# Seven-product (Strassen) matrix products for v and half of z, and the layer norm of v in steps beside the conv projections

## Chip, cores and metric

The kernel runs on one core of one Trainium2 chip. The metric is the device time in microseconds (us) of one execution. The engines are TensorE (PE), VectorE (DVE), ScalarE (ACT), GpSimd (POOL) and SyncE (SP, whose queue issues most loads). Each engine takes its instructions strictly in the order in which they stand in its own list.

## The reference, cut to what matters

One layer over T = 1088 tokens: 1024 rows of a prompt and 64 rows of a sample. All arithmetic is float32.

```
h = RMSNorm(x)
u, v, z, xBC, dt, gate_a, gate_b = split(h @ w_in)      # v: 1024 columns, z: 2048, dt: 32
v   = LayerNorm(gelu(v)) * ln_w + ln_b                  # also an output for the sample rows
o_a = gelu(u) * (W_s v + b)                             # 8 groups of 128 channels, W_s 128 x 128 over positions
xs, B, C = silu(causal_conv(xBC))
y   = SSD(xs, softplus(dt + dt_bias), -exp(a_log), B, C) + D * xs
o_b = GroupRMSNorm(y * silu(z))
x  += RMSNorm((sigmoid(gate_a) * (o_a @ w_a) + sigmoid(gate_b) * (o_b @ w_b)) @ w_out)
x  += RMSNorm(relu(RMSNorm(x) @ w_up)^2 @ w_down)
```

## The kernel before

**Products.** Each float32 operand is split into a high part and a low part (`split`, L79 to L81: ACT copies the source to the high part, `wh`, `hTh`; DVE or POOL subtracts it from the source, which leaves the low part, `wl`, `hTl`). A product of two operands is three matmuls, high x high, high x low and low x high, added in PSUM. `h` stands transposed in SBUF as three column blocks `hT` of 384, 384 and 320 tokens.

**z and v.** `proj_M` (L122 to L134) computes one row tile of 128 tokens by 512 weight columns in 8 x 3 = 24 matmuls of 512 columns. The weights of a column group come as four pieces of 512 KB (`raw`, then `wh`, `wl`). There are nine row tiles; the ninth holds the 64 rows of the sample, and takes 24 matmuls as well. z has four column groups, the loop `for gi in range(1, G)` runs over the last three, and v (`v_part`) has two. A z tile is finished by `sz` on ACT (L344) and DVE (L345) and written to `z_d` in DRAM by POOL's queue (L346). A v tile goes through gelu (`gelu2`, L193 to L196, L214), and in the second half of `v_part` through the layer norm (L219 to L227), and is written to `v_d`.

**dt.** `dt_part` is a generator whose pieces stand between the tiles of z group 1: 72 matmuls give dt for all tokens, nine transposes (L262) turn it, a chain of small DVE and ACT operations (L264 to L285, among them a reciprocal, L276) computes the softplus and times `a`, result `q1`; two matmuls (L289, L292) give its running sums `pcum` and the sums that `toend` is made of.

**After v.** The gate projections (`gate_gen`) and the SSD stage follow. In it, each of four groups projects B, C and xs (`xbc_chunk`: `proj_T`, L118 to L120, 24 matmuls of 384 or 320 columns for each of three token blocks, then the conv: ACT L419 takes PSUM into `raw`, DVE L430 three times, DVE L434 once), and runs the blockwise recurrence. The u projection with the spatial mixing (`spatial`), the branches and the FFN come last; the FFN's products (L966 to L968, L1116 to L1118) are already done by seven products each.

**What sets the order.** The code says what depends on what and how many buffers a tile name has (`bufs`); a scheduler then writes out the list of each engine from estimated times. So code that stands next to each other in a loop is interleaved in the lists, and the lists of before and after are shown below where they matter. Memory of a closed pool is used again by the pool opened next, once all work on the old tiles has ended.

## Time and profile before

| | |
|---|---|
| median of 3 runs (lowest to highest) | 2264.83 us (2264.32 to 2266.65) |
| the profiled execution | 2264.54 us, span 2262.7 us |
| mean granted TensorE clock | 0.992 |
| PE busy | 2193.6 us, 97% |
| PE weight load busy | 1966.6 us, 87% |
| DVE, ACT, POOL busy | 58%, 41%, 36% |
| the chain that ended last | PE 67%, issue 12%, POOL 8%, DVE 5% |

The span runs from the first to the last instruction; the 1.8 us beside it are start and end of the execution. "Busy" is the union of an engine's instructions. The chain that ended last follows the last instruction back to what released it, step by step. The stages, by the names of the rows: z and dt up to about 240 us, v to 337, gates to 361, SSD from there to about 1020, u and spatial mixing to 1140, branches to about 1540, FFN to the end.

### The profile page before, as it was taken

Reading aid. Unit: us, or ns where it says so; the run is one execution under the profiler, and the core shown is the slowest. Engines: PE = TensorE matmul, PEld = TensorE weight load, DVE = VectorE, ACT = ScalarE, POOL = GpSimd, SP = SyncE. Lnnn points to the kernel's source line nnn. Section 1 sums busy time; section 2 is a strip of 40 time slices with the busy share of each in tenths; the row PEclk is TensorE's granted clock in tenths of the full one; section 3 lists DMA queues with packets and bytes.
Section 4 is the critical chain, followed back from the end, with each engine's and each line's share of the span. In section 5 each row is a group of like instructions: output and inputs, shape, how many; then the busy total and the mean of one; then the engine's idle time right before and its main releaser. Section 6 shows DMA issues by size and latency. Waiting matters only on the chain.

```text
span 2262.7 us, 33194 instructions
## 1 busy us (share of the span) xinstructions
PE 2193.6 (97%) x12674; PEld 1966.6 (87%) x12674; DVE 1323.5 (58%) x1850; ACT 924.7 (41%) x1788; POOL 818.9 (36%) x798
## 2 busy tenths in 40 slices
PE   8999999999999989999999999998999998999997
PEld 6777778989979979889999999777999997788786
DVE  5322255677677667655722257377555556577777
ACT  5212255445445455433311133255555555433333
POOL 2010163372472562753322555353222223123134
PEclk9999999999999999999999999999999999999999
DMA  5223123253252342442354445453444447534533
GB/s 183 70 84 109 58 84 115 58 144 97 80 138 81 105 125 69 129 126 76 97 173 130 134 119 166 135 172 114 147 152 148 140 148 244 163 116 131 172 119 114
DMA packets 315464, 281.07 MB, mean 124 GB/s; under 512 B 40043, under 2 KB 281389, under 8 KB 314793
## 3 DMA queue, kind: packets, MB, share of 16 engines
q1 hardware_dynamic: 283336, 240.71, 35.8%
...
q14 instruction: 60, 0.48, 0.1%
...
## 4 chain that ended last, share of the span: by engine, by line
PE 67%; issue 12%; POOL 8%; DVE 5%; DMA 4%; ACT 3%; SPq 0%; ACTq 0%; POOLq 0%; DVEq 0%
PE ps L119 8%; PE ps L118 8%; PE ps L120 8%; PE X L968 3%; PE X L966 3%; PE X L967 3%; PE X L1117 3%; PE X L1118 3%; PE X L1116 3%; PE ps L1117 2%; PE ps L1116 2%; PE ps L1118 2%; DMA raw<-w_branch_b 2%; PE ps L706 2%; PE ps L705 2%
## 5 line engine op out<-in xcount | busy, mean ns | idle before, releaser
L118 PE MATMUL ps<-hTh,wh 128*128 128x384 f32 (+1 forms) x1152 | 384.4, 334 | 5.5 <-ACT raw L419 5.5
L120 PE MATMUL ps<-hTh,wl 128*128 128x384 f32 (+1 forms) x1152 | 386.4, 335 | 0.0
L119 PE MATMUL ps<-hTl,wh 128*128 128x384 f32 (+1 forms) x1152 | 384.5, 334 | 0.0
L81 POOL TENSOR_TENSOR wl<-raw,wh 128x1024 fp32r<-128x1024 f32 x74 | 182.4, 2467 | 270.3 <-ACT wh L80 268.0
L80 ACT ACTIVATE wh<-raw 128x1024 fp32r<-128x1024 f32 x128 | 135.3, 1057 | 268.9 <-PE ps L119 98.2
L118 PEld LDWEIGHTS ps<-hTh,wh 128*128 128x128 f32 x1152 | 217.1, 188 | 11.6 <-ACT raw L419 6.0
L120 PEld LDWEIGHTS ps<-hTh,wl 128*128 128x128 f32 x1152 | 216.9, 188 | 9.8 <-issue 9.7
L119 PEld LDWEIGHTS ps<-hTl,wh 128*128 128x128 f32 x1152 | 217.2, 189 | 7.9 <-issue 7.3
L132 PE MATMUL ps<-wh,hTh 128*128 128x512 f32 (+1 forms) x432 | 171.3, 398 | 1.0 <-ACT hTh L177 0.9
L133 PE MATMUL ps<-wl,hTh 128*128 128x512 f32 (+1 forms) x432 | 170.4, 396 | 0.9 <-DVE wl L81 0.9
L134 PE MATMUL ps<-wh,hTl 128*128 128x512 f32 (+1 forms) x432 | 171.0, 396 | 0.2 <-DVE hTl L178 0.2
L430 DVE SCALAR_TENSOR_TENSOR acc<-raw,cw,acc 128x384 f32<-128x384 f32 (+1 forms) x216 | 134.6, 626 | 33.6 <-ACT acc L428 27.7
L966 PE MATMUL X<-hb,wu 128*128 128x272 f32 x512 | 147.7, 291 | 1.9 <-ACT ev L973 1.0
L967 PE MATMUL X<-hb,wu 128*128 128x272 f32 x512 | 147.6, 289 | 0.3 <-DVE hb L790 0.3
L968 PE MATMUL X<-hb,wu 128*128 128x272 f32 x512 | 146.1, 290 | 0.0
L514 ACT ACTIVATE bc<-bc,pcum 128x128 f32<-128x128 f32 (+1 forms) x288 | 90.8, 384 | 89.3 <-POOL bc L511 88.4
L1110 POOL TENSOR_TENSOR wd<-wd,wd 128x1024 f32<-128x1024 f32 x32 | 85.8, 2684 | 113.6 <-DVE dl L81 74.5
L705 PE MATMUL ps<-ob,wh 128*128 128x384 f32 (+1 forms) x384 | 125.4, 327 | 0.0
L706 PE MATMUL ps<-ob,wl 128*128 128x384 f32 (+1 forms) x384 | 125.4, 327 | 0.0
L704 PE MATMUL ps<-ob,wh 128*128 128x384 f32 (+1 forms) x384 | 125.4, 326 | 0.0
L80 ACT ACTIVATE dh<-wd 128x1024 fp32r<-128x1024 f32 x56 | 59.1, 1055 | 153.2 <-PE ps L1117 91.9
L81 DVE TENSOR_TENSOR dl<-xd,dh 128x1024 fp32r<-128x1024 f32 x56 | 100.4, 1818 | 1.8 <-PE X L968 1.2
...
## 6 DMA issues: line engine op xcount, KB each, us to landing
raw<-w_in SPq DMA_DIRECT2D x72, 512.0 KB, 4.0
xd<-rc_d SPq DMA_DIRECT2D x112, 256.0 KB, 3.9
...
bc<-ac_d SPq DMA_DIRECT2D x64, 256.0 KB, 4.1
raw<-w_branch_b SPq DMA_DIRECT2D x32, 512.0 KB, 4.1
wr<-w_up SPq DMA_DIRECT2D x32, 512.0 KB, 4.1
...
```

The lines of the kernel that those rows point to most:

```text
L80: s.activation(hi, src, AF.Copy)
L81: (lo_eng or v).tensor_tensor(out=lo, in0=src, in1=hi, op=ALU.subtract)
L118: pe.matmul(ps[:, :n], wh[:, k, :], hh[:, k, :n], start=(k == 0), stop=False)
L119: pe.matmul(ps[:, :n], wh[:, k, :], hl[:, k, :n], start=False, stop=False)
L120: pe.matmul(ps[:, :n], wl[:, k, :], hh[:, k, :n], start=False, stop=(k == 7))
L132: pe.matmul(ps[:R, :], hh[:, k, o:o + R], wh[:, kk, :], start=(k == 0), stop=False)
L134: pe.matmul(ps[:R, :], hl[:, k, o:o + R], wh[:, kk, :], start=False, stop=(k == 7))
L705: pe.matmul(ps[:, :n], wh[:, k, :], ob[:, 4 + kk, :], start=False, stop=False)
L706: pe.matmul(ps[:, :n], wl[:, k, :], ob[:, kk, :], start=False, stop=(k == 7))
L966: pe.matmul(ps, wh[:, k, :], bh[:, k, :], start=start and k == 0, stop=False, skip_group_check=chain)
L967: pe.matmul(ps, wh[:, k, :], bl[:, k, :], start=False, stop=False, skip_group_check=chain)
L968: pe.matmul(ps, wl[:, k, :], bh[:, k, :], start=False, stop=k == 3, skip_group_check=chain)
```

## The change

- **z groups 0 and 1** stay as they were, but the sample's tile is done by `sample`: high and low part of the 64 rows stand side by side as 128 columns (`xss`), so that 16 matmuls do what 24 did; the two halves of the result are added after one of them has been moved over by an SP transfer (`sample_out`).
- **v (block 0) and z groups 2 and 3 (block 1)** are 1024 columns each, and become two blocks of seven products in the order P2, P1, P6, P5, P7, P3, P4 (`plan`): the 1024 rows of the prompt are taken as two halves of four row tiles, the depth 1024 and the columns 1024 as two halves each. A product is four row tiles of 12 matmuls, with sums of row tiles (`operand`) on one side and sums of weight quarters (`build`) on the other. P1, P6, P7 and P4 add up in four PSUM tiles `X`. The samples' rows go beside them with `sample`.
- **The sums.** e2, e3 and e4 of the row tiles are built in z group 1 (`sums`: POOL adds, DVE subtractions, `split`), e1 in block 0 (`sum_e1`), written over two halves of `hT`, whose old contents are kept in `b12_d` and loaded back after P7 of block 1. The weight sums are POOL additions of 128 x 1024 pieces (`build`), then split (`prep`).
- **Layer norm** of v: a generator `ln_gen` reads a row tile of `v_d`, normalizes it and writes it back, in steps between the conv projections of xs and at the end of each SSD group. Its weight and bias are applied in `spatial` (one more 128 x 128 matmul for each of 8 chunks), and for the sample's output in `ln_gen` itself with four loads through one buffer (`lo`).
- **dt_part** stands at the start of the SSD stage, its later pieces between the B and C projections of the first group.

The core of the diff:

```diff
...
-        def v_part():
...
-        def dt_part(sp, wk):
...
+        def dt_part(wa, wb_, wc, wd):
...
+        def operand(n, m, x):
+            if n in es:
+                return es[n][x][:, :, m * P:m * P + P]
+            return row_op(*((m, 0), (m, 1), (4 + m, 1), (4 + m, 0))[n], x)
...
+        def sample(ps, j, w, start, stop):
...
+            for q in range(4):
+                wh, wl = (x[:, q % 2, :] for x in w(q // 2))
+                xs_ = xss[:, j * 4 + q, :]
+                if q == 0:
+                    pe.matmul(ps, xs_, wh, start=start, stop=False, skip_group_check=True)
+                pe.matmul(ps[:64], xs_[:, 0:64], wl, start=False, stop=False, skip_group_check=True)
+                if q > 0:
+                    pe.matmul(ps, xs_, wh, start=False, stop=stop and q == 3, skip_group_check=True)
...
+        def build(k, q):
...
+            elif n == "P6":
+                t = kept[b, q] = w_piece(b, 1, 1, q, "v2", True)
+                u = w_piece(b, 0, 0, q, "w11", False)
+                tt_(out=t, in0=t, in1=u, op=ALU.subtract)
+                u = w_piece(b, 0, 1, q, "w12", False)
+                tt_(out=t, in0=t, in1=u, op=ALU.add)
...
+                t = w_piece(b, 1, 0, q, "v4", True)
+                tt_(out=t, in0=t, in1=kept[b, q], op=ALU.subtract)
...
+            def sums(m):
...
+                for x, (i, half) in ((x12, (4 + m, 0)), (x11, (m, 0)), (x22, (4 + m, 1)), (x21, (m, 1))):
+                    g.tensor_tensor(out=x, in0=row_op(i, half, 0), in1=row_op(i, half, 1), op=ALU.add)
+                v.tensor_tensor(out=e1, in0=x12, in1=x11, op=ALU.subtract)
+                v.tensor_tensor(out=e2, in0=x22, in1=e1, op=ALU.subtract)
+                v.tensor_tensor(out=e3, in0=x12, in1=x22, op=ALU.subtract)
+                v.tensor_tensor(out=e4, in0=x21, in1=e2, op=ALU.subtract)
+                for n, e in ((4, e2), (5, e3), (6, e4)):
+                    split(e, operand(n, m, 0), operand(n, m, 1))
...
+            for i in range(NT):
+                z_tile(ws, 1, i)
+                if i in (0, 2, 4, 6):
+                    sums(i // 2)
+                if i in (5, 7):
+                    build(0, (i - 5) // 2)
+                if i == 7:
+                    prep(0, 0)
+            prep(0, 1)
...
+            def sum_e1(m):
...
+                for x, i in ((x12, 4 + m), (x11, m)):
+                    g.tensor_tensor(out=x, in0=row_op(i, 0, 0), in1=row_op(i, 0, 1), op=ALU.add)
+                v.tensor_tensor(out=x12, in0=x12, in1=x11, op=ALU.subtract)
+                split(x12, operand(3, m, 0), operand(3, m, 1))
...
+            todo = [lambda m=m: sum_e1(m) for m in range(4)]
...
+            for k, (b, n) in enumerate(plan):
...
+                for m in range(4):
+                    ps = X[m] if chained else mm.tile([P, 512], F32, tag="mm", name="ps")
+                    mms(ps, XN[n], k, m, n == "P1" or not chained, chained)
+                    if m % 2 == 0:
+                        prep(k + 1, m // 2)
+                    else:
+                        build(k + 2, m // 2)
+                        if todo:
+                            todo.pop(0)()
...
+                    elif n == "P1":
+                        v.tensor_tensor(out=cz[m], in0=ps, in1=cz[m], op=ALU.add)
+                        epi(pm, gelu, cz[m], P, out_rows(b, m, 0), True)
+                    elif n == "P6":
+                        c1[m] = s2("c1")
...
+                    else:
+                        epi(pm, gelu, ps, P, out_rows(b, 4 + m, 0), False)
...
+                if n == "P7" and b == 1:
+                    for d, x in b12_parts():
+                        nc.sync.dma_start(out=x, in_=d)
...
+            def ln_gen():
...
+                for i in (8, 0, 1, 2, 3, 4, 5, 6, 7):
+                    R = ROWS[i]
+                    hs_ = [half("la"), half("lb")]
...
+                        nc.sync.dma_start(out=hs_[f][:R], in_=v_d[i * P:i * P + R, f * 512:f * 512 + 512])
+                    yield
...
+                    for f in range(2):
+                        v.tensor_reduce(out=m[:R, f:f + 1], in_=hs_[f][:R], axis=mybir.AxisListType.X, op=ALU.add)
...
+                    for f in range(2):
+                        v.tensor_scalar(out=hs_[f][:R], in0=hs_[f][:R], scalar1=r[:R], scalar2=None, op0=ALU.mult)
+                        nc.sync.dma_start(out=v_d[i * P:i * P + R, f * 512:f * 512 + 512], in_=hs_[f][:R])
...
+                        for f in range(2):
+                            x = hs_[f]
+                            o = sp.tile([P, 4, P], F32, tag="s4", bufs=1, name="lo").rearrange("p a b -> p (a b)")
+                            for name, op in (("gmlp_ln_w", ALU.mult), ("gmlp_ln_b", ALU.add)):
+                                nc.sync.dma_start(out=o[:R], in_=a[name][0, f * 512:f * 512 + 512].partition_broadcast(R))
+                                v.tensor_tensor(out=x[:R], in0=x[:R], in1=o[:R], op=op)
+                            g.dma_start(out=a["new_gmlp_v_sample"][0, 0][:, f * 512:f * 512 + 512], in_=x[:R])
...
+            dtg = dt_part(wa, wb_, wc, wd)
+            next(dtg)
+            lng = ln_gen()
...
                 for t, th in xbc_chunk(16 + gi, lambda t: sp.tile([P, 384], F32, tag="BT", bufs=3, name="BT")):
                     BT.append(th)
+                    next(dtg, None)
...
+                    next(dtg, None)
...
+                        next(lng, None)
...
+                next(lng, None)
+                next(lng, None)
...
+                pe.matmul(tp[:, 0, :], ones, wt, start=True, stop=True)
+                v.scalar_tensor_tensor(out=bs, in0=tp[:, 0, :], scalar=lnc[:, 8 + c:9 + c], in1=bs, op0=ALU.mult, op1=ALU.add)
...
+                    v.scalar_tensor_tensor(out=q[:, :nf * P].rearrange("p (a b) -> p a b", b=P), in0=sm[:, :nf * P].rearrange("p (a b) -> p a b", b=P),
+                                           scalar=lw, in1=bs.unsqueeze(1).to_broadcast([P, nf, P]), op0=ALU.mult, op1=ALU.add)
...
```

Where instructions move, the lists of the engines show it. The names in them are tile names with a buffer number.

**PE, where `q1` meets `tri`** (the first matmul of the running sums of dt). Before, it stands between two z tiles of group 1:

```order
L132 MATMUL ps_842<-wh_624,hTh1_95 128x512
L133 MATMUL ps_842<-wl_625,hTh1_95 128x512
L134 MATMUL ps_842<-wh_624,hTl1_96 128x512
L289 MATMUL ps_871<-q1_795,tri_657 128x288
L292 MATMUL ps_874<-q1_795,ones_660 128x288
L132 MATMUL ps_880<-wh_606,hTh1_95 128x512
L133 MATMUL ps_880<-wl_607,hTh1_95 128x512
L134 MATMUL ps_880<-wh_606,hTl1_96 128x512
```

After the change the same matmul (now L254, weights `wb__2427`, which holds `q1`) stands in the first SSD group, behind the last token block of the B projection (`ps_2626`) and ahead of the C projection (`ps_2682`):

```order
L121 MATMUL ps_2626<-hTh2_98,wl_2403 128x320
L119 MATMUL ps_2626<-hTh2_98,wh_2402 128x320
L120 MATMUL ps_2626<-hTl2_99,wh_2402 128x320
L121 MATMUL ps_2626<-hTh2_98,wl_2403 128x320
L254 MATMUL ps_2664<-wb__2427,wa_2426 128x288
L257 MATMUL ps_2667<-wb__2427,wa_2426 128x288
L119 MATMUL ps_2682<-hTh0_94,wh_2676 128x384
L120 MATMUL ps_2682<-hTl0_95,wh_2676 128x384
L121 MATMUL ps_2682<-hTh0_94,wl_2677 128x384
L119 MATMUL ps_2682<-hTh0_94,wh_2676 128x384
```

The matmul moved from the z stage to the start of the SSD stage, and everything behind it on PE, the C projection first, comes after it.

**DVE, the chain that ends in `q1`.** Before, between the reciprocal's input and `q1`, DVE's list holds one operation of another kind (L345, z):

```order
L273 TENSOR_SCALAR q1_795<-d1_794 128x288
L274 TENSOR_TENSOR d1_794<-d1_794,q1_795 128x288
L276 RECIPROCAL d1_794<-d1_794 128x288
L345 SCALAR_TENSOR_TENSOR sz_838<-sz_838,ps_813 128x512
L277 TENSOR_TENSOR u1_793<-u1_793,d1_794 128x288
L278 TENSOR_TENSOR u1_793<-u1_793,q1_795 128x288
L279 TENSOR_TENSOR u1_793<-u1_793,e1_792 128x288
L281 TENSOR_TENSOR dtv_102<-dtv_102,u1_793 128x288
L284 TENSOR_TENSOR q1_795<-dtv_102,dtb_662 128x288
L285 MEMSET q1_795 64x32
```

After, with the reciprocal at L241, the conv (L627, L631) and the layer norm (L669) of the same stage stand between its steps:

```order
L239 TENSOR_TENSOR wb__2427<-wb__2427 128x288
L627 SCALAR_TENSOR_TENSOR acc_2615<-raw_2587,cw_2412,acc_2615 128x384
L241 RECIPROCAL wb__2427<-wb__2427 128x288
L631 SCALAR_TENSOR_TENSOR BT_2553<-BT_2553,acc_2548 128x384
L669 TENSOR_REDUCE lm_3205<-lb_3161 128x1
L627 SCALAR_TENSOR_TENSOR acc_2615<-raw_2587,cw_2412,acc_2615 128x384
L242 TENSOR_TENSOR wb__2427<-wb__2427 128x288
L82 TENSOR_TENSOR wl_3121<-raw_3118,wh_3120 128x1024
L627 SCALAR_TENSOR_TENSOR acc_2656<-raw_2624,cw_2412,acc_2656 128x323
L627 SCALAR_TENSOR_TENSOR acc_2615<-raw_2587,cw_2412,acc_2615 128x384
L243 TENSOR_TENSOR wb__2427<-wb__2427 128x288
L627 SCALAR_TENSOR_TENSOR acc_2656<-raw_2624,cw_2412,acc_2656 128x323
```

The chain kept its steps and got neighbours: from its first step (L229) to `q1` (L249) DVE's list holds 9 operations L627, 3 L631, 2 L669, 2 L683, 1 L692, 1 low part of a weight piece (L82) and 3 copies of 3 columns (L613, L619) besides.

**POOL, in block 0.** Before, at the start of v, POOL has one short operation for each tile (L194, gelu) behind the writes of z:

```order
L346 DMA z_d_80<-sz_1579 128x512
L346 DMA z_d_80<-sz_1608 64x512
L194 TENSOR_SCALAR gq_1678<-gq_1678 128x512
L194 TENSOR_SCALAR gq_1710<-gq_1710 128x512
L194 TENSOR_SCALAR gq_1742<-gq_1742 128x512
L194 TENSOR_SCALAR gq_1774<-gq_1774 128x512
L194 TENSOR_SCALAR gq_1806<-gq_1806 128x512
```

After, beside P1 of block 0, row sums (L485), gelu (L316), weight sums (L365, L367) and writes of v (L321) stand there; `v2_1079` is the second half of P6's weights:

```order
L485 TENSOR_TENSOR x_1088<-hTh1_96,hTl1_97 128x512
L485 TENSOR_TENSOR x_1087<-hTh0_94,hTl0_95 128x512
L321 DMA v_d_81<-cz_1015 128x512
L365 TENSOR_TENSOR v2_1079<-v2_1079,w11_1081 128x1024
L485 TENSOR_TENSOR x_1143<-hTh2_98,hTl2_99 128x512
L321 DMA v_d_81<-cz_1045 128x512
L485 TENSOR_TENSOR x_1142<-hTh0_94,hTl0_95 128x512
L485 TENSOR_TENSOR x_1199<-hTh2_98,hTl2_99 128x512
L316 TENSOR_SCALAR t_1174<-t_1174 128x512
L485 TENSOR_TENSOR x_1198<-hTh1_96,hTl1_97 128x512
L367 TENSOR_TENSOR v2_1079<-v2_1079,w12_1084 128x1024
L316 TENSOR_SCALAR t_1206<-t_1206 128x512
```

Between z's last write and the gelu of P1's last tile POOL got 8 row sums, 4 weight sums, 3 gelu operations ahead of the last L367, and 2 writes of v; the piece shows the last 6 row sums and the 2 weight sums of `v2_1079`.

**PE, where P6 of block 0 uses them**: `wh_1113` and `wl_1114` are the first half of the weights, `wh_1169` and `wl_1170` are split from `v2_1079`:

```order
L493 MATMUL X_1099<-wh_1113,e4h_103 128x512
L494 MATMUL X_1099<-wl_1114,e4h_103 128x512
L495 MATMUL X_1099<-wh_1113,e4l_104 128x512
L493 MATMUL X_1096<-wh_1169,e4h_103 128x512
L493 MATMUL X_1097<-wh_1169,e4h_103 128x512
L493 MATMUL X_1098<-wh_1169,e4h_103 128x512
L493 MATMUL X_1099<-wh_1169,e4h_103 128x512
L494 MATMUL X_1096<-wl_1170,e4h_103 128x512
L495 MATMUL X_1096<-wh_1169,e4l_104 128x512
```

All 24 matmuls of the first half of P6 stand ahead of the first one that needs the second half, and P5 comes behind.

## Rows read from the trace of the kernel before

**Rows 1.** The page's busy times: each engine, its busy time, its share of the span, its instructions.

```profile
span 2262.7 us, 33194 instructions
...
PE 2193.6 (97%) x12674; PEld 1966.6 (87%) x12674; DVE 1323.5 (58%) x1850; ACT 924.7 (41%) x1788; POOL 818.9 (36%) x798
```

**Rows 2.** Busy time of each engine by stretch (start and end in us, length, then each engine's busy time with its count of instructions, the granted TensorE clock, the share of the DMA engines and GB/s). The stretches are z from group 1 on with v, the change from gates to SSD, the first conv projections, and most of the SSD stage.

```profile
core 0: us, PE busy (x) PEld busy (x) DVE busy (x) ACT busy (x) POOL busy (x), PEclk, DMA share, GB/s
76.00:346.00 270.00, 269.94 (x1210) 211.91 (x1209) 94.14 (x121) 79.38 (x114) 63.17 (x82) 1.00 0.25 82
346.00:365.00 19.00, 15.90 (x99) 15.64 (x99) 6.08 (x7) 6.13 (x12) 11.11 (x13) 1.00 0.48 152
365.00:455.00 90.00, 87.59 (x539) 84.57 (x539) 58.70 (x104) 45.99 (x107) 27.73 (x35) 0.98 0.26 73
520.00:1020.00 500.00, 484.70 (x2978) 445.16 (x2977) 344.85 (x519) 239.77 (x596) 247.62 (x292) 1.00 0.38 105
```

**Rows 3.** Timeline of POOL in the z stage: start, duration, instruction, idle time before it. These are the writes of one tile position, one column group (nine tiles) apart.

```profile
139.08 0.55 POOL L346 DMA_DIRECT2D z_d<-sz  x1 [5.03 <-DVE sz L345]
...
189.46 0.54 POOL L346 DMA_DIRECT2D z_d<-sz  x1 [5.02 <-DVE sz L345]
```

**Rows 4.** The start of the SSD stage: the timeline of PE (gates up to 360.61, then the B projection), of POOL, and the row of ACT's waits with the time waited, how often, and the longest.

```profile
359.29 0.31 PE L120 MATMUL ps<-hTh,wl 128*128 128x320 f32 x1
...
360.61 0.31 PE L120 MATMUL ps<-hTh,wl 128*128 128x320 f32 x1
364.02 0.44 PE L118 MATMUL ps<-hTh,wh 128*128 128x384 f32 x1 [3.10 <-ACT raw L419]
364.29 0.34 PE L119 MATMUL ps<-hTl,wh 128*128 128x384 f32 x1
...
364.99 0.33 PE L120 MATMUL ps<-hTh,wl 128*128 128x384 f32 x1
...
378.79 0.44 PE L118 MATMUL ps<-hTh,wh 128*128 128x384 f32 x1 [2.41 <-ACT raw L419]
...
359.51 0.55 POOL L230 DMA_DIRECT2D new_gmlp_v_sample<-vst  x1
...
ACT raw L419 <- DMA new_gmlp_v_sample<-vst: 10.9, 1, 10.9
```

**Rows 5.** The dt chain of before, between the tiles of z group 1: the timeline of PE (transposes and the first matmul of the running sums) and of DVE.

```profile
95.09 0.71 PE L262 MATMUL tp<-ident,dtT 32*128 32x32 f32 x9
...
107.02 0.65 PE L289 MATMUL ps<-q,tri 128*128 128x288 f32 x2
...
95.84 0.42 DVE L264 TENSOR_TENSOR dtv<-tp,dtb 128x256 f32<-128x256 f32 x1 [5.76 <-PE tp L262]
...
99.70 1.95 DVE L276 RECIPROCAL d<-d 128x288 f32<-128x288 f32 x1
...
105.35 0.09 DVE L285 MEMSET q<- 64x32 f32 x1
```

**Rows 6.** Groups of instructions by line and shape (busy us, mean ns of one, idle before): the first three from the first conv projections, the next six from z and v, the last from the whole span.

```profile
L430 DVE SCALAR_TENSOR_TENSOR acc<-raw,cw,acc 128x384 f32<-128x384 f32 x36 | 23.4, 662 | 7.7 <-ACT acc L428 6.9
...
L81 DVE TENSOR_TENSOR wl<-raw,wh 128x1024 fp32r<-128x1024 f32 x4 | 5.6, 1398 | 2.8 <-ACT wh L80 2.8
...
L434 DVE SCALAR_TENSOR_TENSOR BT<-BT,acc 128x384 f32<-128x384 f32 x2 | 1.1, 559 | 2.6 <-ACT BT L433 2.6
...
L80 ACT ACTIVATE wh<-raw 128x1024 fp32r<-128x1024 f32 x23 | 24.3, 1059 | 25.1 <-DMA raw<-w_in 17.4 <-PE ps L134 4.2 <-DMA z_d<-sz 3.4
...
L345 DVE SCALAR_TENSOR_TENSOR sz<-sz,ps 128x512 f32<-128x512 f32 x26 | 17.7, 686 | 82.7 <-ACT sz L344 82.7
L227 POOL TENSOR_TENSOR vst<-vst,lnb 128x1024 f32<-128x1024 f32 x7 | 16.9, 2411 | 2.6 <-DVE vst L226 2.6
...
L194 POOL TENSOR_SCALAR gq<-gq 128x512 f32<-128x512 f32 x16 | 12.6, 790 | 43.8 <-ACT gq L193 43.3
...
L344 ACT ACTIVATE sz<-ps 128x512 f32<-128x512 f32 x26 | 15.4, 597 | 114.0 <-PE ps L134 114.0
...
L219 DVE TENSOR_REDUCE mu<-vst 128x1 f32<-128x1024 f32 x8 | 9.8, 1220 | 0.3
...
L868 POOL TENSOR_TENSOR t<-wr 128x512 f32<-128x512 f32 x15 | 19.3, 1290 | 91.8 <-DVE wu L884 86.2 <-PE tp L788 5.6
```

**Rows 7.** Timeline in the FFN's seven-product stage, POOL and then DVE, at the same moments.

```profile
1920.68 5.75 POOL L1110 TENSOR_TENSOR wd<-wd,wd 128x1024 f32<-128x1024 f32 x2 [2.25 <-DVE dl L81]
...
1919.38 1.22 DVE L81 TENSOR_TENSOR dl<-wd,dh 128x1024 fp32r<-128x1024 f32 x1
1920.88 3.28 DVE L81 TENSOR_TENSOR dl<-xd,dh 128x1024 fp32r<-128x1024 f32 x1 [0.28 <-ACT dh L80]
```

**Rows 8.** DMA issues, with KB each and the median us from issue to landing.

```profile
raw<-w_in SPq DMA_DIRECT2D x72, 512.0 KB, 4.0
...
z_d<-sz POOLq DMA_DIRECT2D x26, 256.0 KB, 2.7
```

**Rows 9.** Busy time by stretch as in rows 2: a hand-over and a steady part of the FFN's seven products, and two stretches with a lower granted clock.

```profile
1540.00:1570.00 30.00, 20.81 (x132) 18.51 (x131) 27.80 (x42) 14.67 (x30) 12.71 (x12) 0.89 0.30 99
1570.00:1880.00 310.00, 310.00 (x2467) 310.00 (x2465) 174.25 (x311) 170.00 (x341) 71.59 (x55) 1.00 0.48 146
...
380.00:400.00 20.00, 20.00 (x115) 19.92 (x115) 16.79 (x34) 12.74 (x28) 4.23 (x7) 0.92 0.20 52
...
1910.00:1920.00 10.00, 3.96 (x9) 2.34 (x10) 8.41 (x7) 2.98 (x7) 6.32 (x3) 0.62 0.56 165
```

**Rows 10.** The 128 x 128 matmuls of the spatial mixing, as a group.

```profile
L640 PE MATMUL sm<-wt,vc 128*128 128x128 f32 x128 | 17.0, 274 | 0.0
```

More of the change, by code (lines that the diff above doesn't have):

```diff
@@ L348, in program @@
             first(0)
[L349 to L350 removed]
+            ws = wM_gen(w_in, OFF_Z)
             ws0 = [next(ws)]
```

275 lines of the change are left out of this document (206 added, 69 removed).

## The prediction

> **What bounds the kernel now.** I read the page's busy times first: PE is busy 2193.6 of 2262.7 us [rows 1], so the kernel is a list of matmuls with few gaps, and a change is worth the matmul time that it takes from PE, less the gaps that it makes. Next comes the table by stretch. In z and v, from 76 to 346 us, PE is busy 269.94 of 270 us while DVE has 94, ACT 79 and POOL 63 us of work [rows 2]: nothing there waits. Behind v, from 346 to 365, PE has 15.90 of 19 us, and the timeline shows the gap: PE stops at 360.61 and starts again at 364.02, since ACT's evacuation L419 stands still for 10.9 us, until POOL's last write of v, issued at 359.51, has landed; a second gap of 2.41 us follows at 378.79 [rows 4]. In the first conv projections DVE is already busy 58.70 of 90 us, and in the SSD stage 345 of 500, with PE at 485 [rows 2]. So the z and v stages give back whole what is taken from PE there, and have three other engines nearly free; the stage behind has less room.
>
> A matmul of 512 columns costs PE its distance from the next one, not the duration printed beside it: one column group (nine tiles of 24 matmuls) takes 189.46 - 139.08 = 50.38 us, which is 0.2332 us for each of 216 [rows 3]. In the same way 384 columns take (364.99 - 364.29) / 4 = 0.175 us, and 320 columns (360.61 - 359.29) / 9 = 0.147 us [rows 4].
>
> **The matmuls that go.** A block (1024 columns) took 2 x 9 x 24 = 432 matmuls. It now takes 7 products x 4 tiles x 12 = 336, and four calls of `sample` with 8 each, 368 in all. Two blocks save 128; the sample's tile in z groups 0 and 1 saves 8 each. 144 x 0.2332 = **33.6 us less**. The dt matmuls only move.
>
> **The wait that goes.** The last write of v no longer stands ahead of the conv's first evacuation: 3.1 us less. The second wait of 2.41 us is a backlog of the conv's own ACT work, and I leave it in.
>
> **Wait A, at the start of the SSD stage.** PE's list has the running-sum matmul directly behind the B projection and ahead of the C projection, so PE stops there until `q1` is there. Behind dt's transposes PE has two token blocks left, 24 x 0.175 + 24 x 0.147 = 7.7 us. Before, from the transposes at 95.09 to `q1` at 105.44 the chain took 10.35 us [rows 5], hidden under two z tiles; less two L345 of 0.69 [rows 6], plus some 0.25 to reach PE, its own steps are 9.2 us. Now DVE must also do what stands between the steps: 9 L627 at 0.66 (as L430), 3 L631 at 0.56 (as L434), 2 reductions at half of 1.22, 3 layer-norm operations on 512 columns at most 0.69, one L82 at 1.40 [rows 6], and three tiny copies, some 0.5: 12.8 us. 9.2 + 12.8 - 7.7 = 14.3. I take **13**, since the chain's steps on ACT leave DVE small gaps that the neighbours fill. Bounds: 10, if these gaps take 4; 20, if DVE also sits through two round trips of the `lo` loads (2.7 each by the nearest row [rows 8], and an operation). Queued behind: on PE the C projection, on DVE the conv of C.
>
> **Wait B, in block 0.** Let S0 be the end of the eighth tile of z group 1. PE then has 16 sample matmuls (3.7 us), P2 and P1 with two sample calls (112, 26.1 us), and the first half of P6 (24, 5.6 us), and wants `wh_1169` at S0 + 35.4. The new pool's memory is that of the z stage, free only when the sample's z tile is written: 3.7, ACT 0.6, the SP transfer 2.7, DVE 0.69, ACT 0.6, DVE 0.69, issue 0.54, landing 2.7 [rows 3, 6, 8], with hand-overs S0 + 13. Two row sums fit beside the load of `v2_1030`, 4.0 us [rows 8], until S0 + 17. Then POOL's list has, through the last L367, four weight sums at 2.41, six row sums at 1.29, three gelu steps at 0.79 and two issues at 0.55 [rows 3, 6]: 20.9 us. With ACT's split (1.06) `wh_1169` is there at S0 + 39.0, 3.6 us late. That is with nothing in POOL's way. But two POOL additions beside DVE's took 5.75 us instead of 4.8, and the DVE subtraction beside them 3.28 instead of 1.22 [rows 7]. 20% on 20.9 us are 4.2 more: **8 us** of waiting, between 3.6 and, if each of DVE's fourteen 512-column operations with two SBUF inputs and one of 1.22 delays POOL in full (10.9 us), 14.5. P5's weights come next through the same POOL list.
>
> The Trainium skill, "SBUF — State Buffer", section "Who interferes with whom", says that a VectorE instruction with two SBUF inputs and a GpSimd instruction that reads SBUF exclude each other for a whole instruction. The 3.28 us of [rows 7] agree. By that rule wait B would lie at its upper bound, and the sum 6.5 us higher.
>
> **The rest.** The clock: the old gap left a granted clock of 0.92 over 20 us, 1.6 us lost; after a longer standstill a stretch had 0.62 [rows 9]. Two waits instead of one: **+1.6**. Hand-overs between products: the FFN's seven products run with PE busy 310 of 310 us, but their first 30 us lose 9.2 [rows 9]; here P2 starts with weights that come straight from `w_in`, and I take **+2** (0 to 9). The 8 ones-matmuls and a transpose, of the kind of L640 with 0.27 us of duration [rows 10], somewhat less as distance: **+1**. The layer norm's steps give DVE 9 x 2.6 = 23 us and ACT about as much beside the conv projections of three groups, where DVE has 31 of 90 us free [rows 2]: **+2** (0 to 8). The row sums of `sums` (16 POOL additions of 1.29, 28 DVE operations of 0.69) lie in z group 1, 50 us in which POOL and DVE have little else: nothing, and if that cover were short, e4 would be late for P6, 26 us later. The new loads (28 pieces more) spread over 220 us where the DMA engines are busy 25% [rows 2]: nothing.
>
> **Sum**, against the profiled execution, 2264.5 us (its median is 2264.83, so no shift): 2264.5 - 33.6 - 3.1 + 13 + 8 + 1.6 + 2 + 1 + 2 = **2255.4 us**. With the bounds 10 and 3.6, and no rest but 1, it is 2242; with 20, 14.5 and hand-overs of 5, 2272.
>
> **Rivals.**
> 1. *The gain comes nearly whole.* For it: the FFN's seven products at 310 of 310 us, with POOL additions of 128 x 1024 among them [rows 9]. Then A is the chain alone (9.2 - 7.7 = 1.5), B nothing: 2264.5 - 33.6 - 3.1 + 1.5 + 1 + some 3 = 2233. Against it: DVE takes its list in order, and its neighbours stand in it. Chance 0.20.
> 2. *The sample's layer norm holds DVE.* Its four loads go through one buffer `lo`, each behind the operation before; three of DVE's operations on them stand ahead of dt's first step, the fourth (L692) among its steps. Four round trips of some 3.5 us instead of the part that I count: A is 21, and the sum 2263.5, no change that can be told. For it: a single buffer, SP's queue in order. Against: loads may land while DVE has other rows. Chance 0.15.
> 3. *The change is slower, by DVE and POOL in block 0.* If each of DVE's 20 two-input operations beside POOL (16 of 512 columns, 4 low parts of weights) waits 3.28 - 1.22 = 2.06 us, as in [rows 7], this is 41 us more on DVE, in front of the low parts that PE wants; some 18 us of it hide under P2 and P1, and B becomes about 31: 2278. It decides from a wait B of 22 us on (2269.4). For it: both engines have these operations back to back there, and block 1 repeats the weight sums. Against: POOL's list has gaps, and the FFN lives with the same pair. Chance 0.20.
>
> **How the numbers follow.** My own case, 2245 to 2263, has 0.45. A difference under 0.2% (4.5 us) can't be told from none, so faster means under 2260.3 and slower over 2269.4. Faster: 0.45 less a tail of 0.02, and rival 1: 0.63. Same: the tail and rival 2: 0.17. Slower: rival 3, 0.20. The range leaves out about a half of rival 1 and a half of rival 3: 2234 to 2271. The likeliest case alone: 2245 to 2263.
>
> **What would show it.** The count of 512-column matmuls down by 144, still 0.233 us apart. A gap on PE ahead of the matmul L254, with DVE's `q1` as releaser, of 10 to 20 us, and none of 3.1 at the first conv evacuation. A gap ahead of P6's second half in block 0, released by the high part on ACT or the low part on DVE, with POOL's L367 or L485 ahead of it, 4 to 15 us; POOL's L365 and L367 over 2.4 us, or DVE's L82 at 3 us, if the exclusion counts. No gap of that kind in block 1. The prediction is wrong if PE runs through P6, if the SSD stage from its second group on gets longer by more than 8 us, or if the weight pieces from `w_in` are what PE waits for.

## The result: 0.76% slower, and the profile after

The changed kernel takes 2282.06 us (median of 4 runs, 2279.57 to 2286.60) where the kernel before took 2265.03: a ratio of 1.0076, interval 1.0059 to 1.0094. The prediction was 2255.4 us, within 2234 to 2271: wrong in sign, and outside its range.

The page of the changed kernel, its span and busy times:

```profile
span 2280.5 us, 33458 instructions
...
PE 2173.4 (95%) x12547; PEld 1954.6 (86%) x12547; DVE 1426.2 (63%) x1972; ACT 967.3 (42%) x1875; POOL 901.0 (40%) x861
```

Against [rows 1], PE lost only 20 us of busy time, and the span grew by 18: PE stands still for 107 us instead of 69. DVE has 103 us and POOL 82 us more to do. In the chain that ended last DVE went from 5% to 9%, and DMA from 4% to 8%.

The waits of PE (total, times, longest), those that the kernel before did not have, or under 1 us each:

```profile
PE ps L254 <- DVE wb__2427 L250: 14.1, 1, 14.1
PE X L493 <- ACT wh L81: 9.9, 1, 9.9
...
PE tp L639 <- DVE th L631: 6.1, 5, 2.2
...
PE ps L134 <- DVE wl L82: 4.4, 3, 3.1
...
PE X L493 <- DVE cz L532: 3.7, 1, 3.7
PE ps L219 <- ACT wd L81: 2.4, 1, 2.4
PE ps L133 <- DVE sz L430: 1.9, 1, 1.9
```

L254 is the running sum of dt (wait A of the prediction); L493 is a matmul of the seven products, here in P6 of block 0 (wait B); L134 and L133 have their longest waits in z group 1; L639 is the transpose behind the conv in the SSD stage; L219 is the first dt matmul. Of [rows 4] both waits are gone.

Busy times by stretch (z group 1, then block 0 from P2 to P5):

```profile
core 0: us, PE busy (x) PEld busy (x) DVE busy (x) ACT busy (x) POOL busy (x), PEclk, DMA share, GB/s
60.00:97.00 37.00, 32.03 (x126) 24.65 (x125) 33.54 (x40) 14.03 (x23) 23.16 (x16) 0.91 0.31 93
125.00:185.00 60.00, 45.99 (x181) 35.90 (x180) 43.17 (x33) 20.83 (x32) 38.57 (x26) 0.86 0.52 160
```

In these two stretches, where PE was to be full as in [rows 2], it has 32.03 of 37 and 45.99 of 60 us, and the granted clock is 0.91 and 0.86.

The span by places at which both kernels do the same:

| | before | after | longer by |
|---|---|---|---|
| start to the first gate matmul (z, v) | 336.8 | 315.4 | -21.4, of it -15.0 for dt, which moved out |
| to the first C x B matmul (gates, dt, first conv) | 95.6 | 121.5 | +25.9, of it +15.0 for dt, which moved in |
| to the last C x B matmul (SSD) | 544.8 | 556.3 | +11.5 |
| to the end | 1285.5 | 1287.3 | +1.8 |

The places, in the kernel before and then in the changed one (the first gate matmul, and the C x B matmuls with the starts of the first and the last of them):

```profile
336.80 0.34 PE L118 MATMUL ps<-hTh,wh 128*128 128x384 f32 x1
L503 PE MATMUL cb<-CT,BT x72: 222/274/348, 432.4 to 977.2; 128*128 128x128 f32 x64, 128*64 128x64 f32 x8
...
315.41 0.33 PE L119 MATMUL ps<-hTh,wh 128*128 128x384 f32 x1
L748 PE MATMUL cb<-CT,BT x72: 222/274/422, 436.9 to 993.2; 128*128 128x128 f32 x64, 128*64 128x64 f32 x8
```

The 15.0 us are what seven distances between z's writes in group 1 of the kernel before (73.75 to 127.92 us) exceed 5.6 us each by, summed.

**Why P6 waits.** The timeline of block 0: POOL, DVE, ACT and PE.

```profile
148.98 4.03 POOL L485 TENSOR_TENSOR x<-hTh,hTl 128x512 f32<-128x512 f32 x2
...
153.61 2.38 POOL L365 TENSOR_TENSOR v<-v,w 128x1024 f32<-128x1024 f32 x1
155.94 1.26 POOL L485 TENSOR_TENSOR x<-hTh,hTl 128x512 f32<-128x512 f32 x1
...
163.47 2.79 POOL L367 TENSOR_TENSOR v<-v,w 128x1024 f32<-128x1024 f32 x1
...
167.36 2.66 POOL L371 TENSOR_TENSOR v<-v,w 128x1024 f32<-128x1024 f32 x1
...
153.48 4.27 DVE L486 TENSOR_TENSOR x<-x 128x512 f32<-128x512 f32 x1
...
167.74 2.82 DVE L331 TENSOR_TENSOR sc<-sc,su 64x512 f32<-64x512 f32 x1
170.49 0.68 DVE L320 SCALAR_TENSOR_TENSOR cz<-t,cz 128x512 f32<-128x512 f32 x1
...
171.20 0.63 ACT L315 ACTIVATE t<-sc 64x512 f32<-64x512 f32 x1 [2.72 <-DVE cz L320]
171.74 1.04 ACT L81 ACTIVATE wh<-v 128x1024 fp32r<-128x1024 f32 x1
...
158.41 0.80 PE L493 MATMUL X<-wh,e4h 128*128 128x512 f32 x1 [3.67 <-DVE cz L532]
...
172.83 2.07 PE L493 MATMUL X<-wh,e4h 128*128 128x512 f32 x4 [9.95 <-ACT wh L81]
```

DVE's operations on 512 columns with two inputs in SBUF (L486, L331) take 4.27 and 2.82 us here, instead of the 0.68 of L320 at 170.49, when POOL adds nothing. Beside L486 POOL has a weight sum and a row sum (L365, L485, done at 157.20 us), beside L331 a weight sum of the next product (L371). P6's wait of 3.67 us is for L532, which stands behind L486 in DVE's list. POOL is slowed as well: the two row sums at 148.98 take 4.03 instead of 2.6. At the end POOL is done with P6's weights at 166.26, but ACT's list has the sample's gelu (L315, 171.20) ahead of the split (171.74), and that gelu waits for DVE's L331 and L320.

### The profile page after: what moved, and what is told of

It reads as the page before. It is cut to its first block, busy times and chain, and to the rows that moved or that the text cites. A ratio compares the mean times of both kernels' runs of the same rounds, so it can differ in the third digit from the quotient of the medians.

```text
span 2280.5 us, 33458 instructions
## 1 busy us (share of the span) xinstructions
PE 2173.4 (95%) x12547; PEld 1954.6 (86%) x12547; DVE 1426.2 (63%) x1972; ACT 967.3 (42%) x1875; POOL 901.0 (40%) x861
## 4 chain that ended last, share of the span: by engine, by line
PE 64%; DVE 9%; POOL 8%; DMA 8%; issue 8%; ACT 3%; SPq 0%; ACTq 0%; POOLq 0%; DVEq 0%
PE ps L120 7%; PE ps L119 7%; PE ps L121 7%; PE X L1233 3%; PE X L1231 3%; PE X L1232 3%; PE X L1382 3%; PE X L1383 3%; PE X L1381 2%; PE ps L1381 2%; PE ps L1382 2%; PE ps L1383 2%; PE ps L971 2%; PE ps L970 2%; PE ps L969 2%
## 5 line engine op out<-in xcount | busy, mean ns | idle before, releaser
L82 POOL TENSOR_TENSOR wl<-raw,wh 128x1024 fp32r<-128x1024 f32 x74 | 181.9, 2460 | 249.7 <-ACT wh L81 241.2
L81 ACT ACTIVATE wh<-raw 128x1024 fp32r<-128x1024 f32 x112 | 118.4, 1057 | 254.6 <-PE ps L120 98.5
L627 DVE SCALAR_TENSOR_TENSOR acc<-raw,cw,acc 128x384 f32<-128x384 f32 (+1 forms) x216 | 132.8, 616 | 25.1 <-ACT acc L625 20.6
L82 DVE TENSOR_TENSOR dl<-xd,dh 128x1024 fp32r<-128x1024 f32 x56 | 100.5, 1820 | 4.0 <-DMA rs_d<-C 2.5
L82 DVE TENSOR_TENSOR dl<-wd,dh 128x1024 fp32r<-128x1024 f32 x56 | 72.0, 1292 | 48.9 <-ACT dh L81 47.2
L1382 PE MATMUL X<-dl,dh 128*128 128x512 f32 x256 | 100.4, 395 | 0.0
L1383 PE MATMUL X<-dh,dl 128*128 128x512 f32 x256 | 100.3, 394 | 0.0
```

The costliest lines, as they stand in the source:

```text
L81: s.activation(hi, src, AF.Copy)
L82: (lo_eng or v).tensor_tensor(out=lo, in0=src, in1=hi, op=ALU.subtract)
L1382: pe.matmul(ps, xh, wl, start=False, stop=False, skip_group_check=chain)
L1383: pe.matmul(ps, xl, wh, start=False, stop=q == 3, skip_group_check=chain)
```

## The experiments

All kernels but e8 start from the changed one. A ratio is against the kernel before on the same chip; the changed kernel has 1.0076.

**e1: dt's running sums two token blocks later** (behind the second token block of C, instead of the last of B; the expectation below names the same place, but counts three blocks).

```diff
                     BT.append(th)
-                    next(dtg, None)
+                    if t == 0:
+                        next(dtg, None)
```

> The matmul of dt's running sums (L254) and the transposes behind it move by three token blocks: it stands behind the second token block of C instead of behind the last of B, with 48 more conv matmuls (8.4 us) and a transpose ahead of it. Theory 1 (PE's wait of 14.1 us is the DVE chain, and nothing else is late with it): the wait falls to about 5 us, the time by 8 to 11 us, from 2282 to about 2273. Theory 2 (DVE as a whole is behind, and the chain has more conv neighbours in front of it now): the wait stays over 10 us and the time falls by at most 3 us.

Ratio 1.0027 (1.0015 to 1.0038), 11 us less. PE's wait in e1:

```profile
PE ps L254 <- DVE wb__2427 L250: 5.9, 1, 5.9
```

The wait fell by 8.2 us, nearly the 8.4 us of the 48 matmuls that were put ahead. Theory 1 holds: the chain on DVE hardly changed, 20.3 us from its first step (L229) to `q1` where the changed kernel has 19.5. The other 3 us lie ahead of the gates, which the edit leaves as it was: they start at 311.7 us instead of 315.4.

**e2: the row sums on DVE.**

```diff
-                    g.tensor_tensor(out=x, in0=row_op(i, half, 0), in1=row_op(i, half, 1), op=ALU.add)
+                    v.tensor_tensor(out=x, in0=row_op(i, half, 0), in1=row_op(i, half, 1), op=ALU.add)
...
-                    g.tensor_tensor(out=x, in0=row_op(i, 0, 0), in1=row_op(i, 0, 1), op=ALU.add)
+                    v.tensor_tensor(out=x, in0=row_op(i, 0, 0), in1=row_op(i, 0, 1), op=ALU.add)
```

> The 24 row sums (high + low part of 128 x 512, in z group 1 and in block 0) are done by DVE instead of POOL; the weight sums stay on POOL. Theory 1 (DVE and POOL exclude each other on operations that read SBUF): DVE's two-input operations fall from 1.8 to 4.3 us back to 0.68, the waits of PE in z group 1 (3.1 and 1.9 us) go, that for the second half of P6's weights (9.9 us) falls to under 4, the time by 10 to 15 us to about 2270. Theory 2 (the lists are too full on DVE anyway): 24 x 0.69 = 16.6 us more on DVE keep the waits where they are, and the time stays within 4 us of 2282.

Ratio 1.0019 (1.0007 to 1.0031), 13 us less. In z group 1 the changed kernel's DVE groups (count, busy, mean ns) were:

```profile
L82 DVE TENSOR_TENSOR wl<-raw,wh 128x1024 fp32r<-128x1024 f32 x3 | 6.1, 2020 | 0.0
...
L82 DVE TENSOR_TENSOR e6l<-w,e6h 128x512 fp32r<-128x512 f32 x4 | 3.8, 951 | 0.0
```

and e2 has, below its two stretches as above:

```profile
60.00:97.00 37.00, 37.00 (x164) 29.63 (x163) 31.73 (x51) 15.43 (x25) 3.84 (x7) 1.00 0.32 107
125.00:185.00 60.00, 51.35 (x201) 40.16 (x200) 45.84 (x45) 23.65 (x36) 28.68 (x19) 0.91 0.58 182
...
L82 DVE TENSOR_TENSOR wl<-raw,wh 128x1024 fp32r<-128x1024 f32 x3 | 3.6, 1217 | 0.0
...
L82 DVE TENSOR_TENSOR e6l<-w,e6h 128x512 fp32r<-128x512 f32 x4 | 2.7, 682 | 0.0
```

DVE got ten additions more in this stretch and is busy 31.7 us instead of 33.5; PE is busy 37 of 37 us at full clock. In P6 the wait of 9.9 us for the second half's weights is gone and that of 3.7 fell to 1.9; one of 4.8 for the first half's low part is new (0.4 in the changed kernel). Theory 1 holds, with the weight sums still on POOL.

**e3: no layer norm for the prompt.**

```diff
-                for i in (8, 0, 1, 2, 3, 4, 5, 6, 7):
+                for i in (8,):
```

> The layer norm is left out for the 8 tiles of the prompt (only the sample's tile is normalized), so that o_a of the prompt is wrong; nothing else changes. Theory 1 (the 11.5 us that the SSD stage got longer are the layer norm's steps on DVE and ACT beside the conv): the stretch from the first C x B matmul to the last transpose goes from 580.5 back to about 569 us, PE's waits for the conv's last step (L631, 6.1 us) go, and the time falls by 10 to 12 us to about 2271. Theory 2 (the SSD stage got longer because dt is late and the clock fell): the time falls by at most 4 us.

Ratio 1.0017 (1.0008 to 1.0026), 13 us less. From the first to the last C x B matmul it takes 546.9 us, 9.4 less than the changed kernel and 2.1 more than before; the waits for L631 are gone. The wait for `q1` falls too, to 11.1 us, where the chain has fewer neighbours. Theory 1.

**e4: the sample's gelu behind P6.**

```diff
...
-                s.activation(t[:R], c[:R], AF.Square)
+                if zero is None:
+                    s.activation(t[:R], c[:R], AF.Square)
+                else:
+                    s.activation(t[:R], c[:R], AF.Square, bias=zero[:R])
...
+                elif n == "P6" and gelu:
+                    zero = pm.tile([P, 1], F32, name="zero")
+                    v.tensor_scalar(out=zero, in0=c1[3][:, 0:1], scalar1=0.0, scalar2=None, op0=ALU.mult)
+                    late.pop()(zero)
...
```

> The gelu of the sample's rows in block 0 is made to wait for P6 (its square gets a bias of zero computed from P6's last tile), so that on ACT the split of the second half of P6's weights no longer stands behind it; POOL's list is as before. Theory 1 (ACT, in order, held the finished weight sum back by the 5.4 us between POOL's L367 at 166.3 and ACT's split at 171.7): the wait of 9.9 us falls to about 6, the time by about 4 us to 2278. Theory 2 (POOL or the row sums are what is late): the wait and the time stay within 1 us.

Ratio 1.0078 (1.0062 to 1.0095): nothing gained. PE in P6 of e4:

```profile
170.27 2.08 PE L499 MATMUL X<-wh,e4h 128*128 128x512 f32 x4 [6.47 <-ACT wh L81]
176.98 0.80 PE L500 MATMUL X<-wl,e4h 128*128 128x512 f32 x1 [4.63 <-DVE wl L82]
```

The high part came earlier (the wait is 6.47 instead of 9.95), and then the low part, which DVE makes, was 4.63 us late. The first half of theory 1 came true and the second did not: ACT's order was what PE waited for last, and without it DVE was as late.

**e5: e1 and e2 together.**

> The two edits of e1 and e2 together: dt's running sums three token blocks later, and the 24 row sums on DVE. Theory 1 (the two waits have nothing to do with each other): the gains of 0.49% and 0.57% add up, and the time is about 0.3% under that of the kernel before the change, 2258 beside 2265. Theory 2 (the dt chain is late because DVE carries over work from the products, so that the edits share a cause): the ratio is not under 0.999.

Ratio 0.9990 (0.9978 to 1.0001). The two gains nearly add up: 1.06% under the change would be 0.997. The ratio lies on the border that theory 2 names, so the waits decide: `q1` 6.0 us (5.9 in e1), P6 5.5 and 2.1 (4.8 and 1.9 in e2). Two separate waits, then, with little in common; faster than before can't be told from it. It is the basis of e6.

**e6: the weight sums on DVE as well.**

```diff
-            tt_ = g.tensor_tensor
+            tt_ = v.tensor_tensor
```

> As e5, and the weight sums (12 of 128 x 1024, 8 in block 0's and block 1's second to fifth product each) on DVE too, so that POOL adds nothing up in the products. Theory 1 (what is left of the waits in block 0 of e2, 4.8 + 1.9 + 2.0 us, is still DVE and POOL excluding each other): these fall to under 4 together, the low parts of the weights (L82) take 1.22 again instead of 1.58, and the time falls by a further 3 to 6 us. Theory 2 (DVE is now full: 20 us of work more in some 55 us of block 0 from P2 to P6): the waits stay or grow, and the time is equal to or over that of e5.

Ratio 0.9925 (0.9905 to 0.9945), 14.7 us less than e5, where 3 to 6 were expected. What PE still waited for in P6 of e5 (DVE, POOL, PE):

```profile
139.64 4.24 DVE L485 TENSOR_TENSOR x<-hTh,hTl 128x512 f32<-128x512 f32 x2
143.80 2.82 DVE L317 TENSOR_TENSOR t<-cz,t 128x512 f32<-128x512 f32 x1
...
147.15 1.21 DVE L82 TENSOR_TENSOR wl<-v,wh 128x1024 fp32r<-128x1024 f32 x1
...
143.40 2.68 POOL L367 TENSOR_TENSOR v<-v,w 128x1024 f32<-128x1024 f32 x1
...
148.41 0.80 PE L494 MATMUL X<-wl,e4h 128*128 128x512 f32 x1 [5.51 <-DVE wl L82]
```

The weight sum of this low part was done on POOL at 139.17 us. The low part came 8 us later, since two row sums and L317 ahead of it on DVE took 4.24 and 2.82 us instead of some 1.3 and 0.68 while POOL did the second half's weight sums (L365 from 140.92, L367): 5.1 us, nearly the whole wait. So it was DVE being slowed that was late there, not POOL's own time. The low parts of the weight sums in e5 (z to block 1):

```profile
L82 DVE TENSOR_TENSOR wl<-v,wh 128x1024 fp32r<-128x1024 f32 x16 | 22.4, 1407 | 4.8 <-ACT wh L81 4.8
```

In e6, the stretch of block 0, the same group, PE's waits up to 420 us, and the first gate matmul:

```profile
125.00:185.00 60.00, 58.54 (x253) 46.72 (x252) 49.17 (x64) 29.07 (x44) 17.92 (x15) 1.00 0.69 209
...
L82 DVE TENSOR_TENSOR wl<-v,wh 128x1024 fp32r<-128x1024 f32 x16 | 19.7, 1238 | 0.8 <-ACT wh L81 0.8
...
PE ps L254 <- DVE wb__2427 L250: 4.8, 1, 4.8
PE X L493 <- DVE cz L532: 1.5, 2, 1.2
...
288.25 0.33 PE L119 MATMUL ps<-hTh,wh 128*128 128x384 f32 x1
```

The weight sums are 20, ten in each block, where the expectation has 12: 53 us on POOL in the changed kernel, 25 on DVE here. With all of the sums on DVE, block 0 has 49.17 of 60 us on DVE and 58.54 on PE, and no wait over 1.2 us. Theory 2, that DVE is full, falls. The gates start at 288.25 us, 27.2 earlier than in the changed kernel.

**e7: the products without their sums.**

```diff
...
-                tt_(out=t, in0=t, in1=u, op=ALU.subtract)
...
-                for x, (i, half) in ((x12, (4 + m, 0)), (x11, (m, 0)), (x22, (4 + m, 1)), (x21, (m, 1))):
-                    g.tensor_tensor(out=x, in0=row_op(i, half, 0), in1=row_op(i, half, 1), op=ALU.add)
...
+                for n, (i, half) in ((4, (m, 1)), (5, (4 + m, 0)), (6, (m, 0))):
+                    for x in range(2):
+                        s.activation(operand(n, m, x), row_op(i, half, x), AF.Copy)
...
-            todo = [lambda m=m: sum_e1(m) for m in range(4)]
+            todo = []
```

> The products without their sums: the row sums are replaced by ACT copies of row tiles, the sum e1 and all weight sums are left out with their extra loads, so that v, half of z and what follows from them are wrong. All 736 matmuls of the two blocks stay. Theory 1 (the removed matmuls are worth 33.6 us, and the waits in z and v come from the sums alone): gates start at about 291 us instead of 315, PE's waits between 60 and 300 us are under 4, and the time is 2282 - 23 = 2259. Theory 2 (the transition of memory from the z stage to the products, or the products' own hand-overs, hold PE): waits of over 8 us stay there, and the time is over 2267.

Ratio 0.9944 (0.9929 to 0.9959), 2254.6 us. The two stretches, and the first gate matmul:

```profile
60.00:97.00 37.00, 37.00 (x164) 29.56 (x163) 11.23 (x16) 8.78 (x13) 3.85 (x7) 1.00 0.34 107
125.00:185.00 60.00, 60.00 (x262) 48.50 (x261) 35.50 (x46) 29.01 (x44) 13.27 (x19) 1.00 0.53 167
...
286.33 0.33 PE L119 MATMUL ps<-hTh,wh 128*128 128x384 f32 x1
```

PE is full in both, and the gates start at 286.3 us. Against 336.8 of before that is 50.5 us, less dt's 15.0: 35.5 us for the matmuls that went, where 33.6 were predicted. Not all of it need be the 144: the matmuls that stay are 0.230 us apart in z group 1 here, not 0.2332. Theory 1 holds, which put the gates at 291. The sums with their loads, then, cost the changed kernel 315.4 - 286.3 = 29.1 us (25 to 29, since e1 and e3, which leave this part as it is, reach the gates at 311.7 and 313.9). In e6, with every load and every sum, but the sums on DVE, the gates start only 1.9 us later than here. So nearly the whole 29.1 us are the price of where the sums ran, not of the sums, the loads or the hand-overs.

**e8: in the kernel before, the sample's tile of z alone.**

```diff
...
+                if i == 8:
+                    ps = mm.tile([P, 512], F32, tag="mm", name="ps")
+                    for k in range(8):
+                        wh, wl = (x[:, k % 2, :] for x in ws[k // 2])
...
+                        pe.matmul(ps[:64], xss[:, k, 0:64], wl, start=False, stop=False, skip_group_check=True)
...
```

> The kernel before, with one part of the change alone: the sample's tile of the four z groups is done with high and low part side by side, 16 matmuls instead of 24. Theory 1 (a matmul that goes from a stage without waits gives 0.2332 us): 32 x 0.2332 = 7.5 us less, 2257.5. Theory 2 (the transfer that moves half of the result, or the additions, hold a PSUM buffer or the next group's pieces): less than 3 us.

Ratio 0.9963 (0.9949 to 0.9977): 8.4 us (5 to 12 by the interval), theory 1. This part of the change is worth its matmuls without any sums.

**e9: e6 with dt one token block later still.**

> As e6 (row sums and weight sums on DVE), with dt's running sums one token block later still, behind the whole C projection: 24 matmuls of 320 columns more (3.5 us) ahead of L254. Theory 1 (the wait of 4.8 us for q1 in e6 is a chain of fixed length): it falls to about 1.3 us, the time by 3 to 4 us against e6 (ratio 0.991). Theory 2 (what PE doesn't wait for q1 it waits for the conv's last step, since DVE is behind as a whole): waits for L631 grow by as much, and the ratio stays at 0.9925.

Ratio 0.9909 (0.9892 to 0.9925), 2245.14 us: the fastest complete version here, 1.7% under the changed kernel and 0.9% under the one before. The wait for `q1` is 2.5 us instead of 4.8, and 1.5 us more of waiting for L631 came in its place ahead of 420 us. Against e6 the two intervals overlap, so neither theory is decided.

**e10: more room behind the layer norm's loads** (e9 with one `yield` more between the load and the sums).

> As e9, with one step more between the load of a layer-norm tile and its first use, so that DVE's list has a whole conv block between them. Theory 1 (the layer norm's price of 11 us is DVE and ACT standing in order behind loads that have not landed, 11.5 us in e6): DVE's waits for la fall to under 3 us, PE's waits for L631 (7.6 us) to under 4, and the time falls by 3 to 6 us against e9. Theory 2 (the price is the work of the layer norm itself beside a conv that DVE and ACT just keep up with): no difference over 2 us to e9.

Ratio 0.9940 (0.9923 to 0.9957): slower than e9. PE's waits for the conv, and DVE's for the load:

```profile
PE tp L639 <- DVE th L631: 11.3, 8, 2.8
...
DVE lm L670 <- DMA la<-v_d: 10.5, 6, 2.9
```

Both theories fall, the first by sign: DVE's waits for `la` did not go (9.2 us in e9), PE's for the conv grew from 7.2 to 11.3, and the time grew by 7 us where theory 2 allowed 2. Where the scheduler put the room in DVE's list is not shown.

**e11: POOL writes where it added.**

```diff
...
-                    g.tensor_tensor(out=x, in0=row_op(i, half, 0), in1=row_op(i, half, 1), op=ALU.add)
+                    g.memset(x, 0.0)
+                    g.memset(x, 0.0)
+                    v.tensor_tensor(out=x, in0=row_op(i, half, 0), in1=row_op(i, half, 1), op=ALU.add)
...
```

> As e2 (the 24 row sums on DVE), but POOL first writes zeros twice into each sum's tile, so that POOL's list and the order of the steps (POOL, then DVE) are as in the change, with operations that write SBUF and read nothing. Theory 1 (what slows DVE is that both read SBUF): DVE's operations in z group 1 stay at 0.68 us, PE has no wait there, and the time is that of e2 within 4 us (ratio 1.000 to 1.004). Theory 2 (POOL's place in the order is what is late, whatever it does): the waits of the change come back (3 and 2 us in z group 1, over 8 in P6), and the ratio is 1.005 or more.

Ratio 1.0002 (0.9990 to 1.0015), that of e2. Z group 1:

```profile
60.00:97.00 37.00, 37.00 (x163) 29.36 (x162) 32.22 (x51) 15.16 (x24) 13.61 (x27) 1.00 0.33 107
...
L440 POOL MEMSET w<- 128x512 f32 x10 | 5.3, 556 | 0.0
...
L82 DVE TENSOR_TENSOR wl<-raw,wh 128x1024 fp32r<-128x1024 f32 x3 | 3.6, 1210 | 0.0
...
L82 DVE TENSOR_TENSOR e6l<-w,e6h 128x512 fp32r<-128x512 f32 x4 | 2.7, 681 | 0.0
```

POOL is busy 13.6 us in the same places of its list (two memsets take 1.1 us, an addition 1.29), and DVE's operations keep 1.21 and 0.68 us. The longest wait in P6 is 3.8 us. Theory 1 holds: what slowed DVE in z group 1 is an operation of POOL that reads SBUF, not POOL's work as such.

**e12: the layer norm's sums and scalings on ACT** (e9 as basis).

```diff
...
-                        v.tensor_reduce(out=m[:R, f:f + 1], in_=hs_[f][:R], axis=mybir.AxisListType.X, op=ALU.add)
...
+                        s.activation(jm[:R], hs_[f][:R], AF.Copy, accum_out=m[:R, f:f + 1])
...
-                        v.tensor_scalar(out=hs_[f][:R], in0=hs_[f][:R], scalar1=r[:R], scalar2=None, op0=ALU.mult)
+                        s.activation(hs_[f][:R], hs_[f][:R], AF.Identity, scale=r[:R])
...
```

> As e9, with the layer norm's sums and scalings of 512 columns (4 operations for each tile, 36 in all) on ACT instead of DVE, so that DVE has no layer-norm operation beside the conv but the sample's. Theory 1 (DVE's share, 9 x 2.3 us of work and the waits for la in its list, is what holds the conv's last step): PE's waits for L631 (7.2 us) fall under 3, and the time falls by 5 to 9 us against e9, ratio 0.987 to 0.989. Theory 2 (ACT's list is what holds it, since DVE's longest waits there are for ACT's tanh, L630): 36 operations of 0.6 more on ACT make it longer by 3 to 10 us, ratio over 0.992.

Ratio 0.9926 (0.9903 to 0.9950), not better than e9:

```profile
PE tp L639 <- DVE th L631: 8.1, 6, 3.3
...
ACT jm L670 <- DMA la<-v_d: 10.9, 6, 2.8
```

PE waits as long for the conv, and ACT now stands behind the loads where DVE stood. Theory 1 falls. The ratio fits theory 2, but its interval overlaps that of e9: that ACT's list is what costs is possible, and not shown.

**e13: e9 without the layer norm of the prompt.**

> As e9, with the layer norm left out for the 8 tiles of the prompt, so that o_a of the prompt is wrong. Theory 1 (the layer norm costs the SSD stage some 10 us whatever the rest does): the time falls by 8 to 12 us against e9, ratio about 0.986. Theory 2 (in e3 most of the gain was the shorter start, where the dt chain shared DVE with it): under 4 us.

Ratio 0.9855 (0.9839 to 0.9871), 0.54% or 12 us under e9. The SSD stretch is 543.8 us instead of 555.9. Theory 1: the layer norm costs that stage 9.4 us (e3) to 12.1 us (here), with the sums on POOL or on DVE. The price lies where its operations stand: from the first C x B matmul of the first group to that of the second, with four tiles of the prompt between, e9 takes 10 us longer than e13 (168.3 and 158.2), to the third 2 us, and behind it nothing.

## Why the prediction was wrong, step by step

| step | predicted | measured |
|---|---|---|
| matmuls that go | -33.6 | -35.5 (e7) |
| sums: wait B, hand-overs, most of the clock | +8, +2, part of +1.6 | +29.1 (changed kernel less e7) |
| start of the SSD stage without dt's own time: wait A, less the old wait | +13 - 3.1 | +10.9 |
| layer norm beside the conv | +2 | +11.5 (9.4 by e3, 12.1 by e13) |
| spatial mixing and the rest | +1 | +1.8 |

**Right:** the matmuls (1152 of 512 columns in z and v instead of 1296), and wait A, 14.1 us where 13 were forecast, by the chain that was counted out (e1 moved it by the time put ahead); that it came so near is in part luck, see rival 2. The old wait of 3.1 us went, and with it the second of 2.41, which I had left in; in its place came 2.4 us for dt's weights (L219).

**Wrong, first: wait B and what lies around it.** "20% on 20.9 us" put the exclusion of DVE and POOL on POOL alone, and on one wait. It lies on DVE more: in block 0 the means of L320, L486, L82 (row parts) and L317 were 1.86, 1.81, 1.60 and 1.22 us instead of 0.68, which is 15 us in 16 operations, and every low part behind them came late. P6 waited 0.4 + 3.7 + 9.9 us. The same happened where I wrote "nothing": in z group 1, with POOL and DVE both at the row sums, 3.1 and 1.9 us of waits, the second in part by way of POOL, which was held up there itself:

```profile
79.23 10.95 POOL L439 TENSOR_TENSOR w<-hTh,hTl 128x512 f32<-128x512 f32 x4 [4.78 <-DVE w L442]
```

Four row sums took 10.95 us instead of 5.2. Then the clock: behind the waits of 3.1, 1.9, 3.7 and 9.9 us PE's matmuls stand 0.43 us apart instead of 0.23, the lower of its two levels (1.2 instead of 2.4 GHz), for some 16 us together. That is some 8 us lost, an estimate from these distances; I had 1.6 in all. P6's three waits and these two (19.0 us) and the clock make some 27 of the 29.1 us. The hand-overs, +2, were nothing of their own: e7 has PE at 60 of 60 us in block 0. e2, e6 and e11 show the cause directly: the same sums on DVE, more work for the engine that was already the busier one, took the waits away, and write-only work of POOL in place of the row sums did no harm. The Trainium skill, "SBUF — State Buffer", section "Who interferes with whom", says just that: VectorE with two SBUF inputs contends with a GpSimd instruction that reads SBUF, not with one that only writes it. The runs agree on both halves: up to 4.27 us beside additions, 0.68 beside memsets. I gave that rule 6.5 us.

**Wrong, second: the layer norm at +2.** I compared its 23 us of DVE work with DVE's free time (31 of 90 us). It cost 9.4 to 12.1 us: PE waited for the conv's last step (L631) 6.1 us, and without the layer norm not at all (e3). DVE and ACT take the conv's steps in turn, and operations of the layer norm stand between them in their lists, some of them behind a load; that this order is the cause is argued, not shown. Why, in detail, stays open: more room in the code (e10) and its 36 operations of 512 columns on ACT (e12) did not bring it back. The prediction's own sign for this, over 8 us from the second SSD group on, did not show it: that part grew by 3.5 us (from 386.1 to 389.6), the rest lies ahead of the second group.

**The rivals.** Rival 3 (0.20) named the mechanism and, at 2278 us, nearly the time, but not the sizes: it put 41 us on DVE in one wait, where some 15 us were lost in block 0 and the rest came from z group 1, the clock and the layer norm; that its time was nearly met is luck. Rival 1's time, 2233, is met only by e13 (2235), with the sums on DVE and without the layer norm of the prompt, so not by a complete kernel. Rival 2 happened in part: L692 stood 2.9 and 2.6 us behind loads of `lo`, and the chain's first step came at 349.74 us, 2.4 us after the transposes were done. From there it took 19.5 us where I had counted 20.7 (13 and the 7.7 of PE's two token blocks), so two errors of mine nearly cancel in the 14.1.
